# A two-layer hybrid decoder on one core: the products with w1 and w3 by one level of Strassen's scheme, and the first layer's FFN features in two parts

## The chip, the cores and the metric

The kernel runs on one core of a Trainium2 chip. The time is that of one execution on the device in microseconds (us). Engines: PE is TensorE (matrix products), DVE is VectorE, ACT is ScalarE, POOL is GpSimd, SP is SyncE, which issues the transfers (DMAs) between device memory and SBUF. Products land in PSUM.

## What is computed

Two hybrid decoder layers over T = 528 tokens (16 meta tokens and 512 real ones), 1024 features wide. What the change touches is the feed-forward network (FFN) of each layer, 2816 hidden features; the mixing ahead of it (retention, pooling, forgetting attention) stays.

```python
def hybrid_layer(h, w_in, ..., w_out, ln1_g, ln1_b, w1, w3, w2, ln2_g, ln2_b, cos, sin):
    ...
    mix = jnp.einsum('ble,ed->bld', mix, w_out)
    h = layer_norm(ALPHA * h + mix, ln1_g, ln1_b)

    a = jnp.einsum('bld,df->blf', h, w1)
    b = jnp.einsum('bld,df->blf', h, w3)
    y = jnp.einsum('blf,fd->bld', jax.nn.silu(a) * b, w2)
    return layer_norm(ALPHA * h + y, ln2_g, ln2_b)
```

## The kernel before

Activations lie with features on the 128 partitions and tokens along the columns: eight tiles (k = 0 to 7) of 128 features. The tokens are split into half A (272 columns: meta tokens and the first 256) and half B (256). Every fp32 operand is split into a high part (ACT's cast) and a low part (the tile minus its high part, by `sub_lo`, L137 and L138, on DVE or POOL), and a product is three matmuls: high weight with high tile, high with low, low with high (`mm3`, L195 to L197).

Weights come in chunks of 128 x 1024 (512 KB) in the order in which they are used. `fetch` issues the transfer into one of three `raw` buffers; `ensure` has ACT cast it (L174) and DVE or POOL subtract it (L138) into one of four `w` buffers. SP issues all transfers in order.

The FFN's hidden stage (`ffn_hidden`, L973) goes through 22 feature tiles f. Each has two units, one with w1 and one with w3, of eight k tiles each, and each unit is done for half A and half B: 24 matmuls per unit and half. A unit's result is one PSUM buffer `acc`, of which there are two. After a w1 unit ACT takes the Silu (L981); after a w3 unit DVE multiplies (L984), ACT casts the gate to its high part (L986), DVE subtracts the low part. In layer 0 all units go by halves of 272 and 256 columns; in layer 1 the first four units (f = 0 and 1) go by halves of 256, and the rest by 512 columns at once. The first four units do half A before any does half B (A0 to A3, B0 to B3), since half B's layer norm (DVE L334 and L335, ACT L269, casts L271, POOL low parts) is still running when half A's units begin.

After layer 0's hidden stage (262 to 520.6 us of the span) come the products with w2 over all 22 feature tiles, then the second layer norm and layer 1; after layer 1's (885 to 1143 us) the products with w2 for the output (`w2b`). For residual and output the layer norm's result is added up again from its two parts on POOL (`whole`, L355, the operation at L361).

PE's program order is written out: `Plan` picks among pieces by priority and by estimated delays (LAG). The order on the other engines comes from a list scheduler, and every engine runs its queue in order.

Of the kernel before, what the change touches and what calls it, by code (L numbers as in the profile page):

```python
# [43 lines left out]
class Piece:  # L44
    """A run of TensorE work (with what the other engines do on it), placed by Plan."""
# [59 lines left out]
def hymba_kernel(ctx: ExitStack, tc: tile.TileContext, d: dict, out: bass.AP):  # L105
# [16 lines left out]
    # ---------------------------------------------------------------- helpers  # L122
# [17 lines left out]
    # ------------------------------------------------------------ constants in  # L140
# [8 lines left out]
    users = {}  # L149
# [19 lines left out]
    def ensure(upto):  # L169
        while len(loaded) < len(chunks) and len(loaded) <= upto:  # L170
            fetch(len(loaded))
            raw, (_, n, eng) = raws[len(loaded)], chunks[len(loaded)]
            w = wp.tile([P, 2, 1024], F32R, tag="w", name="w")
            nc.scalar.copy(w[:, 0, :n], raw[:, :n])  # L174
# [24 lines left out]
    def unit(u, xs, ks, n, evac, ahead, prio, deps_k):  # L199
        """one output tile: the chunks u of the weights against the tiles xs(), over the k in ks; its last piece."""  # L200
# [3 lines left out]
        for i in range(0, len(ks), q):  # L204
            part = ks[i:i + q]

            def fn(i=i, part=part):
# [13 lines left out]
            for c in {u[k // 8] for k in part}:  # L221
                deps += users.get(c - 4, [])
# [4 lines left out]
            for c in {u[k // 8] for k in part}:  # L227
                users.setdefault(c, []).append(prev)
# [3 lines left out]
    def stage(units, xs, ks, n_of, evac, deps_k, head=0, halves="AB", ahead=2, prio=9):  # L232
        """units: (chunk ids, key); the first `head` units do half A before any does half B.
        Returns the last pieces by (key, half)."""
        done = {}
        i = 0
        while i < len(units):
            g = head if i < head else 1
            for half in halves:
                for u, key in units[i:i + g]:  # L240
# [4 lines left out]
                        lambda k, half=half, key=key: deps_k(half, key, k))  # L245
# [1046 lines left out]
```

## Time and profile before

| | us |
|---|---|
| median of 3 runs | 1273.67 (1272.68 to 1273.88) |
| the profiled execution: its span | 1271.5 |
| that execution with what lies around the span: taken as the median | 1273.7 (2.2 around it) |
| PE busy | 1234.6 |
| DVE, ACT, POOL busy | 646.6, 479.9, 337.7 |

A row of the timeline gives start, duration (us), engine, line, operation, output<-inputs, shape; at its end, in brackets, how long the engine had been idle before it and who released it. A row of windows gives the stretch, its length, then busy time and number of instructions of PE, PE's weight loads, DVE, ACT and POOL, the granted clock of PE, the share of the DMA engines and GB/s. Grouped rows give count, busy time and mean duration in ns; a row of transfers gives count, KB each and the median time from issue to landing. Some matmul records are missing from a trace.

### The profile page before, as it was taken

The page shows a single profiled execution, that of the slowest core. Times are in us where ns is not written, and L with a number is a line of the kernel's source. Part 1 is how long each engine was busy: PE and PEld are TensorE (multiplying, and loading weights), DVE is VectorE, ACT ScalarE, POOL GpSimd, SP SyncE. Part 2 cuts the span into 40 slices and gives each one's busy share as a digit, 9 for nine tenths or more (in the row PEclk, how much of TensorE's full clock was granted, in tenths as well). Part 3 has the DMA queues.
Part 4 walks back from the last instruction along what each step waited for, and adds up shares of the span by engine and source line. Part 5 has one row for each costly group of instructions (what it writes and reads, how often), then busy time and mean ns, then how long its engine had stood idle before and what let it go on. Part 6 is the DMA issues. An engine that isn't in the chain of part 4 may idle for free. (4 is left out here: it accounts for less than half of the span.)

```text
span 1271.5 us, 21413 instructions
## 1 busy us (share of the span) xinstructions
PE 1234.6 (97%) x8650; PEld 1145.8 (90%) x8650; DVE 646.6 (51%) x1257; ACT 479.9 (38%) x893; POOL 337.7 (27%) x375
## 2 busy tenths in 40 slices
PE   7999999889999999999999999998999999999997
PEld 6999989889999999999999899997888888888886
DVE  7575677963333333333384756789632333332226
ACT  5436544543232232222264366455423232221112
POOL 5423339740001100010055243498600000000004
PEclk9999999999999999999999999999899999999999
DMA  6431212423222223233343221134222232222222
GB/s 231 125 99 51 68 34 101 135 98 100 96 88 86 98 84 96 77 90 92 108 143 123 80 80 59 34 118 153 94 84 99 85 99 95 88 100 100 99 91 75
DMA packets 41506, 122.58 MB, mean 96 GB/s; under 512 B 6392, under 2 KB 12696, under 8 KB 41408
## 3 DMA queue, kind: packets, MB, share of 16 engines
q1 hardware_dynamic: 41408, 121.22, 29.1%
q8 instruction: 68, 1.11, 0.4%
q14 instruction: 30, 0.25, 0.1%
HBM read 115.22 MB, written 2.10 MB: 92 GB/s over the span
## 5 line engine op out<-in xcount | busy, mean ns | idle before, releaser
L195 PE MATMUL acc<-xh,w 128*128 128x256 f32 (+2 forms) x1920 | 589.7, 307 | 0.4 <-DVE ka L138 0.4
L196 PE MATMUL acc<-xl,w 128*128 128x256 f32 (+2 forms) x1920 | 582.0, 303 | 1.5 <-POOL xl L138 1.0
L197 PE MATMUL acc<-xh,w 128*128 128x256 f32 (+2 forms) x1920 | 581.8, 303 | 0.0
L138 DVE TENSOR_TENSOR w<-raw,w 128x1024 fp32r<-128x1024 f32 (+1 forms) x181 | 217.4, 1203 | 332.7 <-ACT w L174 332.4
L195 PEld LDWEIGHTS acc<-xh,w 128*128 128x128 f32 x1920 | 363.4, 189 | 18.1 <-issue 1.6
L196 PEld LDWEIGHTS acc<-xl,w 128*128 128x128 f32 x1920 | 364.1, 190 | 16.4 <-POOL xl L138 1.9
L197 PEld LDWEIGHTS acc<-xh,w 128*128 128x128 f32 x1920 | 363.1, 189 | 13.7
L174 ACT CAST w<-raw 128x1024 fp32r<-128x1024 f32 (+1 forms) x211 | 218.8, 1038 | 301.7 <-PE acc L197 121.1
L138 POOL TENSOR_TENSOR w<-raw,w 128x256 fp32r<-128x256 f32 (+1 forms) x74 | 120.6, 1635 | 69.7 <-ACT w L174 61.7
L361 POOL TENSOR_TENSOR y<-xh,xl 128x256 f32<-128x256 f32 (+1 forms) x64 | 51.2, 827 | 225.2 <-DVE g8Bl L138 93.8
L256 POOL TENSOR_TENSOR r<-r,mhalf 128x1 f32<-128x1 f32 (+3 forms) x18 | 14.7, 819 | 324.6 <-DVE r L255 324.6
L138 POOL TENSOR_TENSOR xl<-y,xh 128x256 fp32r<-128x256 f32 (+1 forms) x57 | 49.6, 886 | 22.3 <-ACT xh L271 16.3
L981 ACT ACTIVATE y<-acc 128x272 f32<-128x272 f32 (+1 forms) x44 | 17.2, 392 | 89.0 <-PE acc L197 89.0
L981 ACT ACTIVATE sa<-acc 128x512 f32<-128x512 f32 (+1 forms) x24 | 13.5, 563 | 88.4 <-PE acc L197 88.4
L984 DVE TENSOR_TENSOR sa<-sa,acc 128x512 f32<-128x512 f32 (+1 forms) x24 | 15.4, 642 | 59.0 <-PE acc L197 57.9
L285 DVE SCALAR_TENSOR_TENSOR y<-y,acc 128x256 f32<-128x256 f32 (+1 forms) x48 | 20.1, 420 | 44.5 <-PE acc L197 44.3
L984 DVE TENSOR_TENSOR y<-y,acc 128x272 f32<-128x272 f32 (+1 forms) x44 | 18.9, 429 | 40.4 <-PE acc L197 40.4
L290 POOL TENSOR_TENSOR y<-y 128x256 f32<-128x256 f32 (+1 forms) x12 | 11.0, 914 | 106.3 <-DVE y L285 106.3
L294 ACT ACTIVATE y<-y 128x256 f32<-128x256 f32 (+1 forms) x42 | 17.6, 419 | 54.6 <-DVE y L285 54.5
L680 ACT ACTIVATE p<-p,sm 128x144 f32<-128x144 f32 (+3 forms) x48 | 27.6, 574 | 17.7 <-DVE sm L679 16.1
L683 POOL TENSOR_SCALAR pm<-p,sm 128x16 f32<-128x16 f32 x48 | 21.8, 455 | 43.8 <-DVE sm L681 42.5
L290 DVE TENSOR_TENSOR y<-y 128x256 f32<-128x256 f32 (+1 forms) x30 | 32.1, 1071 | 2.5 <-POOL y L290 1.2
(1000 smaller groups left out, 1916.9 us busy)
## 6 DMA issues: line engine op xcount, KB each, us to landing
raw<-in_w SPq DMA_DIRECT2D x88, 512.0 KB, 3.3
raw<-in_w_in SPq DMA_DIRECT2D x42, 512.0 KB, 4.0
raw<-in_w_out SPq DMA_DIRECT2D x32, 512.0 KB, 3.4
raw<-in_w2b SPq DMA_DIRECT2D x22, 512.0 KB, 3.3
raw<-in_w2a SPq DMA_DIRECT2D x18, 512.0 KB, 3.4
raw<-in_w2a SPq DMA_DIRECT2D x9, 384.0 KB, 3.2
xin<-in_x SPq DMA_DIRECT2D x4, 512.0 KB
out<-y SPq DMA_DIRECT2D x12, 128.0 KB, 1.8
```

Source lines behind the costliest of these rows:

```text
L138: return eng.tensor_tensor(lo, full, hi.bitcast(F32), op=ALU.subtract)
L174: nc.scalar.copy(w[:, 0, :n], raw[:, :n])
L195: nc.tensor.matmul(ps, lhsT=wh, rhs=hi, start=first, stop=False)
L196: nc.tensor.matmul(ps, lhsT=wh, rhs=lo, start=False, stop=False)
L197: nc.tensor.matmul(ps, lhsT=wl, rhs=hi, start=False, stop=last)
L285: nc.vector.scalar_tensor_tensor(y, y, ALPHA, ps, op0=ALU.mult, op1=ALU.add)
L290: (nc.gpsimd if CFG[f"s{i}"] else nc.vector).tensor_tensor(self.s, self.seen[0] if i == 1 else self.s, y, op=ALU.add)
L361: nc.gpsimd.tensor_tensor(y, hi[:, o:].bitcast(F32), lo[:, o:].bitcast(F32), op=ALU.add)
L680: nc.scalar.activation(out=p[:, :NM + nk], in_=p[:, :ce], func=AF.Exp, scale=-1.0, bias=sm[:, 0:1], accum_out=sm[:, 1:2])
L683: nc.gpsimd.tensor_scalar(F[c, "pm"][:, h, :], p[:, :NM], sm[:, 2:3], 1.0, op0=ALU.mult, op1=ALU.mult)
L981: nc.scalar.activation(out=s, in_=ps, func=AF.Silu)
L984: nc.vector.tensor_tensor(s, s, ps, op=ALU.mult)
```

## The change

For feature tiles f = 3 to 21 of both layers, w1 and w3 of one feature tile are taken together as a 2 x 2 block matrix: w1 and w3 are its two rows, the first four and the last four k tiles its columns. The tokens are the second matrix: first and last half of the k tiles by first and last half of the tokens (264 columns each in layer 0, 256 in layer 1). One level of Strassen's scheme (in Winograd's form) makes the four results from seven products of four k tiles each, so 7 x 4 x 3 = 84 matmuls per feature tile where there were 96 of the same width (48 of 512 columns in layer 1).

It needs sums of weights per feature tile (`sums_of`: s1 to s4, with their own high and low parts), sums of tokens once per layer (`factors`: T1 to T4) and sums of products (in `fast`). The seven products lie in three PSUM banks: bank 0 is `acc`, banks 1 and 2 are `one`. Bank 1 is used three times over: product 2 (s2 T2), product 4 (s3 T3) added to it, and product 6 (A22 T4) added to that, each after the reading of what was there.

```diff
+KH = KF // 2
+HEAD = 3
...
+            if eng == "S2":
+                loaded.append(sums_of(raws[len(loaded) - 1], raw, loaded[-1], w))
+                continue
...
+    def sums_of(a1, a2, w1, w2):
...
+        v.tensor_tensor(raw[1], a2[:, a], a2[:, b], op=ALU.add)
+        v.tensor_tensor(raw[2], raw[1], a1[:, a], op=ALU.add)
+        v.tensor_tensor(raw[4], raw[2], a1[:, b], op=ALU.add)
+        v.tensor_tensor(a2[:, a], a2[:, a], a1[:, a], op=ALU.add)
+        for i in (2, 1):
+            nc.scalar.copy(s[i][:, 0], raw[i])
+        nc.scalar.copy(w2[:, 0], a2)
+        nc.scalar.copy(s[4][:, 0], raw[4])
+        sub_lo(v, w1[:, 1], a1, w1[:, 0])
+        for i in (2, 1):
+            sub_lo(v, s[i][:, 1], raw[i], s[i][:, 0])
+        sub_lo(v, w2[:, 1], a2, w2[:, 0])
+        sub_lo(nc.gpsimd, s[4][:, 1], raw[4], s[4][:, 0])
...
+    def factors(k, n, hs, Th, Tl):
...
+        for p, c0, c1 in second(k):
+            v.tensor_tensor(o[1][:, c0:c1], b11[:, c0:c1], p, op=ALU.subtract)
+        for p, c0, c1 in second(k + 4):
+            v.scalar_tensor_tensor(o[0][:, c0:c1], o[1][:, c0:c1], -1.0, p, op0=ALU.mult, op1=ALU.subtract)
+        for (p, c0, c1), (q, _, _) in zip(second(k), second(k + 4)):
+            v.tensor_tensor(o[2][:, c0:c1], q, p, op=ALU.subtract)
+        v.scalar_tensor_tensor(o[3], o[0], -1.0, b21, op0=ALU.mult, op1=ALU.subtract)
+        for i in range(4):
+            nc.scalar.copy(Th[:, k, i], o[i])
+            sub_lo(v if i % 2 else nc.gpsimd, Tl[:, k, i], o[i], Th[:, k, i])
+
+    PRODUCTS = (("A11", "B11", 0), ("s2", "T2", 1), ("s1", "T1", 2), ("s3", "T3", 1), ("A12", "B21", 0), ("A22", "T4", 1),
+                ("s4", "B22", 2))
...
+            def evac(i, f=f, bank=bank, t=t):
+                a, b, c = (bank[j][:, :n] if j in bank else None for j in range(3))
+                if i == 0:
+                    t["p1"], t["u3"] = home(f)
+                    nc.scalar.copy(t["p1"], a)
+                elif i == 1:
+                    t["u2"] = slot(n)
+                    v.tensor_tensor(t["u2"], t["p1"], b, op=ALU.add)
+                elif i == 3:
+                    u = t["u3"]
+                    v.tensor_tensor(u, t["p1"], b, op=ALU.add)
+                    v.tensor_tensor(u, u, c, op=ALU.add)
+                elif i == 4:
+                    t["s"] = slot(n)
+                    nc.scalar.activation(out=t["s"], in_=a, func=AF.Silu)
+                elif i == 5:
+                    v.tensor_tensor(t["p1"], t["p1"], b, op=ALU.add)
+                    gated(f, 0, t["s"], t["p1"])
+                elif i == 6:
+                    v.tensor_tensor(t["u2"], t["u2"], c, op=ALU.add)
+                    nc.scalar.activation(out=t["u2"], in_=t["u2"], func=AF.Silu)
+                    gated(f, 1, t["u2"], t["u3"])
...
+        def split(f, c0, c1, t):
+            hi, lo = (g[:, c0:c1] for g in gt[f])
+            nc.scalar.copy(hi, t)
+            sub_lo(nc.gpsimd if f >= HEAD else nc.vector, lo, t, hi)
...
+        def gated(f, j, s, u):
+            nc.vector.scalar_tensor_tensor(u, s, -1.0, u, op0=ALU.mult, op1=ALU.mult)
+            split(f, N * j, N * (j + 1), u)
...
+        for i, fs in enumerate((range(KH), range(KH, KF))):
...
+            last = fast(l, fs[0 if i else HEAD:], 0, N, Th, Tl, yslot, lambda f: (yslot(N), yslot(N)), gated, [(sums[-1], LAG["T"])], prev)
```

Feature tiles 0 to 2 stay as they were, though in layer 1 all three now go by halves of 256. In layer 0 the hidden stage and its w2 products are cut in two parts: tiles 0 to 10 and their w2 products, then tiles 11 to 21 and theirs, added to the first. Seven chunks more are transferred for the same bytes. The layer norm's results stay in SBUF as fp32, so that `whole` is gone from the FFN. Layer 1's gates are kept as fp32 and split into parts in the last stage, one feature tile at a time.

The order on DVE in a steady part of layer 0, one feature tile before the change (two PSUM readings at L984, the gate's low parts, two weight chunks):

```order
L984 TENSOR_TENSOR y<-y,acc 128x272 [waits PE_49]
L138 TENSOR_TENSOR g13Al<-y,g13Ah 128x272 [waits Activation_49]
L984 TENSOR_TENSOR y<-y,acc 128x256 [waits PE_49]
L138 TENSOR_TENSOR w<-raw,w 128x1024 [waits DMAHW5_49,Activation_49]
L138 TENSOR_TENSOR g13Bl<-y,g13Bh 128x256 [waits Activation_49]
L138 TENSOR_TENSOR w<-raw,w 128x1024 [waits DMAHW6_49,PE_49,Activation_49]
```

The same after the change, most of a feature tile: L1068 is the reading of product 6, L1071 of product 7, L1059 of the next tile's product 2; L1135 are the gates, L140 the low parts (`w` of A11 with A12 and of s3 with A22, `S` of s1 and s2), L192 to L195 the weight sums. The row behind the last one is L1062, the reading of the next tile's product 4.

```order
L1068 TENSOR_TENSOR y<-y,one 128x264 [waits PE_49]
L140 TENSOR_TENSOR w<-raw,w 128x1024 [waits Activation_49]
L1135 SCALAR_TENSOR_TENSOR y<-y 128x264 [waits DVE_49]
L140 TENSOR_TENSOR w<-raw,w 128x1024 [waits Activation_49]
L1071 TENSOR_TENSOR y<-y,one 128x264 [waits PE_49]
L140 TENSOR_TENSOR S<-sr,S 128x512 [waits Activation_49]
L1135 SCALAR_TENSOR_TENSOR y<-y 128x264 [waits Activation_49]
L1059 TENSOR_TENSOR y<-y,one 128x264 [waits PE_49]
L192 TENSOR_TENSOR sr<-raw 128x512 [waits DMAHW1_49,DVE_49]
L140 TENSOR_TENSOR S<-sr,S 128x512 [waits Activation_49]
L195 TENSOR_TENSOR raw<-raw 128x512 [waits DMAHW0_49,DVE_49]
L193 TENSOR_TENSOR sr<-sr,raw 128x512 [waits DVE_49]
```

Where six instructions stood per feature tile, fifteen stand, five of which read PSUM for PE's next product. POOL, which had nothing per tile there, gets two low parts of gates and that of s4 in layer 0, and that of s4 alone in layer 1.

At the head of layer 0's hidden stage, ACT's order before around the Silu of unit A2 (y_3568; the xh rows are half B's high parts, g0Ah the high part of the first gate):

```order
L986 CAST g0Ah_3329<-y_3461 128x272 [waits DVE_49]
L269 ACTIVATE y_2657<-y_2657,c_pv_96 128x256 [waits DVE_49]
L269 ACTIVATE y_2659<-y_2659,c_pv_96 128x256 [waits DVE_49]
L271 CAST xh_84<-y_2657 128x256 [waits Activation_49]
L981 ACTIVATE y_3568<-acc_3538 128x272 [waits PE_49]
L269 ACTIVATE y_2661<-y_2661,c_pv_96 128x256 [waits DVE_49]
```

The same Silu after the change (y_3580); Th are the high parts of T1 to T4:

```order
L1029 CAST Th_3329<-y_3484 128x264 [waits DVE_49]
L1029 CAST Th_3329<-y_3487 128x264 [waits DVE_49]
L1029 CAST Th_3329<-y_3504 128x264 [waits DVE_49]
L1029 CAST Th_3329<-y_3503 128x264 [waits DVE_49]
L1029 CAST Th_3329<-y_3505 128x264 [waits DVE_49]
L1029 CAST Th_3329<-y_3506 128x264 [waits DVE_49]
L1029 CAST Th_3329<-y_3523 128x264 [waits DVE_49]
L1029 CAST Th_3329<-y_3524 128x264 [waits DVE_49]
L1029 CAST Th_3329<-y_3522 128x264 [waits DVE_49]
L1109 ACTIVATE y_3580<-acc_3550 128x272 [waits PE_49,Pool_49]
L1029 CAST Th_3329<-y_3525 128x264 [waits DVE_49]
```

It has moved from the middle of half B's layer norm to behind all of it and fourteen casts of T. PE's order there is as before; the first unit of half B takes the `acc` buffer that this Silu reads:

```order
L228 MATMUL acc_3582<-xh_84,w_3559 128x272
L226 MATMUL acc_3615<-xh_84,w_3264 128x256 [waits Activation_49]
L227 MATMUL acc_3615<-xl_85,w_3264 128x256 [waits Pool_49]
L228 MATMUL acc_3615<-xh_84,w_3264 128x256
L226 MATMUL acc_3615<-xh_84,w_3264 128x256
```

The first row is the end of unit A3, the second the first matmul of B0. On PE nothing has moved here; what its wait stands for has.

More of the change, by code (lines that the diff above doesn't have):

```diff
@@ L230, in unit, with stage @@
         return prev
-    def stage(units, xs, ks, n_of, evac, deps_k, head=0, halves="AB", ahead=2, prio=9):
+    def stage(units, xs, ks, n_of, evac, deps_k, head=0, halves="AB", ahead=2, prio=9, k0=0):
         done = {}
@@ L965, in mixing @@
             ap = norm.finish([done[m, half] for m in range(KD)], base, base + 8, xn)
-            om.holds("y", KD, ap[-1])
+            keep[half] = [Piece(None, 0.0, [], 0) for _ in range(2)]
+            for p in keep[half]:
+                om.holds("y", KD // 2, p)
             for k in range(KD):
@@ L974, in ffn_hidden @@
+    def ffn_hidden(l, slot, put):
         sa = {}
@@ new lines, in put, with room @@
+        def put(f, half, s, ps):
+            nc.vector.tensor_tensor(s, s, ps, op=ALU.mult)
+            split(f, *((0, NA) if half == "A" else (NA, T)), s)
+        def gated(f, j, s, u):
+            nc.vector.scalar_tensor_tensor(u, s, -1.0, u, op0=ALU.mult, op1=ALU.mult)
+            split(f, N * j, N * (j + 1), u)
+        def room(fs):
+            for f in fs:
+                gt[f] = [gp.tile([P, T], F32R, tag=f"g{f % KH}{s}", name=f"g{f}{s}") for s in "hl"]
+        room(range(KH))
+        us, evac = ffn_hidden(l, yslot, put)
@@ L1005, in ffn_mid @@
-        end = [done[us[-1][1], h] for h in "AB"]
-        us, dn = list(zip(w2_u[l], (*range(KD), KD - 2))), {}
-        norm = {h: Norm(h, n_of[h], hs, f"f{l}") for h in "AB"}
-        for part, halves in ((us[:6], "AB"), (us[6:7], "A"), (us[7:8], "AB"), (us[8:], "B")):
-            dn.update(stage(part, lambda half: [gt[f, half] for f in range(KF)], list(range(KF)), lambda h, key: n_of[h],
-                            lambda m, half, ps: norm[half].evac(m, ps),
-                            lambda half, key, k: [gdone[k, half], wh] + end, halves=halves, ahead=1))
+        sums = [plan.add(lambda k=k: factors(k, N, hs, Th, Tl), 0.0, [ready["A", KD - 1][0], ready["B", KD - 1][0]], 5) for k in range(4)]
@@ new lines, in ffn_mid, with evac2 @@
+        gdone = {f: [(done[(f, 1), h], LAG["g"]) for h in "AB"] for f in range(HEAD)}
+        prev = done[us[-1][1], "B"]
+        dn = {}
+        norm = {h: Norm(h, n_of[h], hs, f"f{l}", 1.0) for h in "AB"}
+        def evac2(m, half, ps):
+            y = hs[half][m]
+            nc.vector.scalar_tensor_tensor(y, y, ALPHA, ps, op0=ALU.mult, op1=ALU.add)
+        for i, fs in enumerate((range(KH), range(KH, KF))):
+            if i:
+                prev = plan.add(lambda: room(range(KH, KF)), 0.0, end, 9)
+            last = fast(l, fs[0 if i else HEAD:], 0, N, Th, Tl, yslot, lambda f: (yslot(N), yslot(N)), gated, [(sums[-1], LAG["T"])], prev)
+            gdone.update({f: [(p, LAG["g2"])] for f, p in last.items()})
+            end = [last[fs[-1]]]
+            us = list(zip(w2_u[i], (*range(KD), KD - 2)))
+            for part, halves in ((us[:6], "AB"), (us[6:7], "A"), (us[7:8], "AB"), (us[8:], "B")) if i else ((us, "AB"),):
+                dn.update(stage(part, lambda half, fs=fs: {f: tuple(g[:, :NA] if half == "A" else g[:, NA:] for g in gt[f]) for f in fs},
+                                list(fs), lambda h, key: n_of[h],
+                                lambda m, half, ps, i=i: norm[half].evac(m, ps) if i else evac2(m, half, ps),
+                                lambda half, key, k, end=end: gdone[k] + end, halves=halves, ahead=1, k0=fs[0]))
+            end = [dn[us[-1][1], h] for h in "AB"]
@@ L1029, in ffn_last @@
                      lambda half, key, k: [ready[half, k]], head=4)
-        done.update(stage(us[4:], lambda half: both, list(range(KD)), lambda h, key: 2 * NB, evac,
-                          lambda half, key, k: [ready[h, k] for h in half], halves=("AB",)))
-        ht, hw = {}, {}
+        sums = [plan.add(lambda k=k: factors(k, NB, hw, Th, Tl), 0.0, [ready["A", KD - 1][0], ready["B", KD - 1][0]], 5) for k in range(4)]
+        last = fast(l, range(HEAD, KF), NM, NB, Th, Tl, sa, lambda f: (g[f][:, :NB], g[f][:, NB:]), gated, [(sums[-1], LAG["T"])], done[us[-1][1], "B"])
@@ L1034, in turn @@
+        ht = {}
         def turn(half, b, q):
-            if b == 0 and q == 0:
-                hw[half] = whole(x, half, 256)
             tp = one()
@@ L1071, in part @@
             nc.tensor.matmul(ps, lhsT=lo, rhs=wh, start=False, stop=last_)
+        for k in range(3):
+            split(k)
         KT = 4
         for k in range(KF - KT):
-            ensure(w2_u[l][k][0] + 2)
+            ensure(w2_u[-1][k][0] + 2)
+            split(k + 3)
             for b in range(4):
@@ L1083, in ffn_last @@
             nc.sync.dma_start(gb[j], d["gb"][:, j, :])
-        fo = [gp.tile([P, 512], F32, tag="sa", name="fo", bufs=3) for _ in range(2)]
+        fo = [gp.tile([P, 512], F32, tag="sr", name="fo", bufs=3) for _ in range(2)]
         def sums(b, st, q):
```

197 lines of the change are left out of this document (133 added, 64 removed).

## The prediction

> **What bounds the kernel now.** I read the page's table of engines first, then the row of granted clock, then the windows of the two hidden stages that the change touches.
>
> ```profile
> span 1271.5 us, 21413 instructions
> PE 1234.6 (97%) x8650; PEld 1145.8 (90%) x8650; DVE 646.6 (51%) x1257; ACT 479.9 (38%) x893; POOL 337.7 (27%) x375
> PEclk9999999999999999999999999999899999999999
> ...
> 250.00:520.00 270.00, 266.46 (x2168) 265.64 (x2168) 107.44 (x165) 87.51 (x155) 31.12 (x34) 0.99 0.28 93
> 900.00:1140.00 240.00, 240.00 (x1123) 198.01 (x1122) 85.19 (x101) 77.24 (x121) 14.80 (x18) 1.00 0.28 92
> ```
>
> TensorE (PE) is busy for 97% of the span at full clock, and in the two FFN hidden stages for 266.46 of 270 us and for all of 240 us (first pair of figures of a window). VectorE (DVE) is at 107.44 and 85.19 us there. So fewer matmuls shorten these stages, but only until VectorE, which gets the new additions, is late instead. What a matmul costs is read from the Silu instructions, one after each w1 unit:
>
> ```profile
> 301.22 0.40 ACT L981 ACTIVATE y<-acc 128x272 f32<-128x272 f32 x1 [1.62 <-PE acc L197]
> 304.05 0.39 ACT L981 ACTIVATE y<-acc 128x256 f32<-128x256 f32 x1 [2.43 <-PE acc L197]
> 312.93 0.40 ACT L981 ACTIVATE y<-acc 128x272 f32<-128x272 f32 x1 [1.62 <-PE acc L197]
> ...
> 922.61 0.60 ACT L981 ACTIVATE sa<-acc 128x512 f32<-128x512 f32 x1 [4.23 <-PE acc L197]
> 933.73 0.60 ACT L981 ACTIVATE sa<-acc 128x512 f32<-128x512 f32 x1 [4.01 <-PE acc L197]
> ```
>
> Layer 0: 312.93 - 301.22 = 11.71 us for one feature tile, that is 96 matmuls of 272 and 256 columns, 0.122 us each at a mean of 264. The 24 matmuls of 256 columns between the first two rows take 2.83 us, 0.118 each. Layer 1: 11.12 us for 48 matmuls of 512 columns, 0.232 each.
>
> **What the change removes.** For 19 of 22 feature tiles per layer, 84 matmuls of 264 (layer 0) or 256 columns (layer 1) stand for 96. That is 84 x 0.122 = 10.25 us, 1.46 less; and 84 x 0.118 = 9.91 us, 1.21 less. If TensorE never waits: 19 x 1.46 + 19 x 1.21 = 50.7 us. Feature tile 2 of layer 1 stays plain but moves to 256 columns: 96 x 0.118 - 11.12 = 0.2 us dearer. The two parts of w2 hold the same matmuls, and the seven more SP transfers move the same bytes; I cost both at nothing, since the weights for them are prepared under products that last longer than their casts (up to 1 us at each of two joints if not).
>
> The PSUM banks make one chain per feature tile. Product 6 (A22 T4) needs bank 1, which VectorE must have read after product 4 (L1062); the next thing that VectorE does for TensorE waits for product 6 (L1068); and until the next L1062 it has thirteen instructions in its order, L1068 itself among them: four of 264 columns that read PSUM, two gates of 264 in SBUF, two subtractions of 1024, five operations of 512. Their durations:
>
> ```profile
> 311.03 1.23 DVE L138 TENSOR_TENSOR w<-raw,w 128x1024 fp32r<-128x1024 f32 x1 [0.70 <-ACT w L174]
> 312.17 0.42 DVE L138 TENSOR_TENSOR g3Bl<-y,g3Bh 128x256 fp32r<-128x256 f32 x1
> ...
> 930.38 0.68 DVE L138 TENSOR_TENSOR g2l<-sa,g2h 128x512 fp32r<-128x512 f32 x1
> ...
> 272.02 0.43 DVE L138 TENSOR_TENSOR g0Al<-y,g0Ah 128x272 fp32r<-128x272 f32 x1
> 272.37 0.41 DVE L335 TENSOR_TENSOR y<-y,one 128x256 f32<-128x256 f32 x1
> 272.70 0.41 DVE L334 TENSOR_TENSOR y<-y,one 128x256 f32<-128x256 f32 x1
> ```
>
> In a queue the next instruction starts 0.08 us before the end of the one ahead (311.03 + 1.23 against 312.17). So 1024 columns cost 1.14, 512 cost 0.60, 264 cost 0.34 (0.35 at 272, 0.33 at 256). Sum: 6 x 0.34 + 2 x 1.14 + 5 x 0.60 = 7.3 us, and 0.4, my estimate, for dependent neighbours and extra semaphores. Then product 6: 12 x 0.122 = 1.46, and from its last matmul to a reader:
>
> ```profile
> 312.60 0.29 PE L197 MATMUL acc<-xh,w 128*128 128x272 f32 x1
> ...
> 910.58 0.38 ACT L981 ACTIVATE sa<-acc 128x256 f32<-128x256 f32 x1
> ...
> 911.01 0.38 PE L195 MATMUL acc<-xh,w 128*128 128x256 f32 x1
> ```
>
> The Silu of 312.93 starts 0.33 us after its last matmul starts, 0.20 after that one's turn of 0.122; and a matmul starts 0.05 us after the reader that it waits for (910.58 + 0.38 against 911.01). The loop so far: 7.7 + 1.46 + 0.25 = 9.4 us in layer 0 and 9.3 in layer 1, **shorter than TensorE's 10.25 and 9.91**. What decides is GpSimd (POOL), which gets three subtractions per tile in layer 0 (264, 264 and 512 columns) and one of 512 in layer 1:
>
> ```profile
> 910.65 2.44 POOL L361 TENSOR_TENSOR y<-xh,xl 128x256 f32<-128x256 f32 x2
> 911.34 1.75 POOL L361 TENSOR_TENSOR y<-xh,xl 128x256 f32<-128x256 f32 x1
> ...
> 910.71 1.78 DVE L138 TENSOR_TENSOR w<-raw,w 128x1024 fp32r<-128x1024 f32 x1 [3.40 <-ACT w L174]
> 912.41 0.41 DVE L984 TENSOR_TENSOR sa<-sa,acc 128x256 f32<-128x256 f32 x1
> 912.74 1.43 DVE L138 TENSOR_TENSOR w<-raw,w 128x1024 fp32r<-128x1024 f32 x1
> ...
> 270.27 0.75 POOL L138 TENSOR_TENSOR xl<-y,xh 128x256 fp32r<-128x256 f32 x1 [5.05 <-ACT xh L271]
> L138 POOL TENSOR_TENSOR w<-raw,w 128x1024 fp32r<-128x1024 f32 x28 | 68.8, 2460 | 13.0 <-ACT w L174 13.0
> ```
>
> Beside GpSimd a VectorE subtraction of two SBUF tiles took 1.78 and 1.43 us instead of 1.23, and GpSimd's own took 1.75 instead of 0.75. The second GpSimd row ends at 913.09, 0.60 after VectorE's 912.49: they take turns, and a turn of GpSimd is 0.60 for 256 columns. VectorE's L984 between them, which reads PSUM, kept its 0.41. With 0.75 for 256 and 2.46 for 1024, GpSimd's 512 is about 1.3, its turn about 1.15 (estimate). In layer 0 that is 0.61 + 0.61 + 1.15 = 2.4 us per tile, in layer 1 1.15. How much lies beside VectorE's four PSUM readings, no row shows: between nothing and all of it is added. A reading is 0.34 long and a turn 0.6 or more, so at most half of a small turn hides behind one; I take 1.8 and 1.15 as exposed. **Loops: 11.2 us in layer 0, 10.5 in layer 1** (ends 10.25 to 11.8, 9.91 to 10.7; weight transfers add to layer 1's upper end, since w chunks landing after 4.0 instead of 3.3 us come late for L192 by up to 0.4).
>
> ```profile
> raw<-in_w SPq DMA_DIRECT2D x88, 512.0 KB, 3.3
> raw<-in_w_in SPq DMA_DIRECT2D x42, 512.0 KB, 4.0
> ```
>
> The loop holds only where weights are prepared two tiles ahead: 15 tiles of layer 0, 17 of layer 1; the last two of each of the three runs of tiles go at TensorE's rate. Saved: 15 x 0.5 + 4 x 1.46 + 17 x 0.6 + 2 x 1.21 = 26 us, less 0.2 for tile 2 and about 1.5 where the runs fill: **24 us**.
>
> **What it adds.** T1 to T4 are made at the head of each hidden stage, between the layer norm's last steps for half B. Before, that head runs without a stop:
>
> ```profile
> 268.35 0.42 DVE L335 TENSOR_TENSOR y<-y,one 128x256 f32<-128x256 f32 x1 [1.95 <-PE one L329]
> ...
> 272.13 0.40 ACT L981 ACTIVATE y<-acc 128x272 f32<-128x272 f32 x1
> ...
> 274.83 0.29 PE L197 MATMUL acc<-xh,w 128*128 128x272 f32 x1
> 274.95 0.28 PE L195 MATMUL acc<-xh,w 128*128 128x256 f32 x1
> ```
>
> The Silu at 272.13 reads unit A2 and frees the PSUM buffer that the first unit of half B takes at 274.95. In the changed order fourteen casts of T stand ahead of this Silu on ACT, the last of them behind VectorE's 15 PSUM operations (0.33), 12 of 256 columns and 9 of about 264 (0.34) and nine small ones (estimate 0.1): 5.0 + 4.1 + 3.1 + 0.9 = 13.1, with 1.0 for dependent neighbours 14 us from 268.35, so 282.4, then cast and Silu (0.4 each) and 0.25: B starts at 283.4 at the earliest, 8.5 us late. GpSimd has about 13 subtractions in that time, 0.6 a turn, 7.8 if none hides: 16 us late at most. I take 12. What is queued behind the Silu on ACT are g1's cast, the next weight cast and B's Silus, and TensorE waits for all of them through that one buffer. A stop costs clock as well:
>
> ```profile
> 892.00:896.00 4.00, 4.00 (x17) 3.71 (x18) 2.34 (x8) 0.38 (x1) 1.17 (x2) 0.50 0.31 118
> 896.00:900.00 4.00, 4.00 (x28) 3.95 (x27) 2.67 (x8) 0.55 (x2) 4.00 (x7) 0.78 0.00 0
> ...
> 891.95 0.66 PE L312 MATMUL one<-c_ident,y 128*128 128x128 f32 x2 [4.24 <-DVE y L290]
> ```
>
> After 4.24 us of idle the granted clock (seventh figure) was 0.50 for 4 us and 0.78 for 4 more: 4 x 0.5 + 4 x 0.22 = 2.9 us lost; I take 2.5. In layer 1 the A2 Silu keeps its early place, but B0's Silu (910.58 before) comes behind eleven T casts and a weight cast. The same VectorE work from 899 gives 912.5, with turns and casts about 914; B2 starts 3.5 us late (1 to 6), and half a clock step after it, 1.5. Heads together: 12 + 2.5 + 3.5 + 1.5 = **19.5 us** (11 to 28). The 32 additions that GpSimd no longer makes (L361) and the splitting of layer 1's gate inside the last stage lie beside TensorE either way, and I cost them at nothing.
>
> **Sum.** 1271.5 + 2.2 around it is the median of 1273.7. 1273.7 - 24 + 19.5 = **1269**, own range 1260 to 1280, chance 0.50.
>
> **Rivals.** *TensorE stays the bound* (0.22): at most 0.85 us of GpSimd's turns is exposed in layer 0, 0.6 in layer 1, the rest beside PSUM readings and waits. Then 1273.7 - 50.5 + 19.5 = 1243. For it: the unslowed 0.41 of 912.41. Against: nine of the loop's thirteen instructions, the longest among them, read two SBUF tiles.
>
> *VectorE and GpSimd queue for each other in full* (0.20), the slower side: a turn is GpSimd's whole duration, 0.75 + 0.75 + 1.3 = 2.8 in layer 0 and 1.3 in layer 1, none hidden; loops 12.2 and 10.6; saved -7.4 + 5.8 + 8.8 + 2.4 - 1.7 = 8; the layer 0 head stops 16 us: 1273.7 - 8 + 23.5 = 1289. It decides against the change from loops of about 11.3 and 10.7 on, where 24 falls to 19.5. For it: 1.78 instead of 1.23 from a single GpSimd operation; against: the 0.60 above. The Trainium skill (SBUF — State Buffer, Who interferes with whom) calls the pair of ports that these two share an exclusive lock, held for the whole instruction, and taken by a VectorE instruction with two SBUF inputs; by that rule this rival is the forecast, 1289, and the rows bear out the turns but not their full length.
>
> *Matmuls in three banks go slower than in one* (0.03): at 0.14 us each 84 of them take the old 11.7, so only the cost stays, 1293. Against it: 512 columns cost 0.232 and 256 cost 0.118, so the pitch goes by columns. The Trainium skill (TensorE: Matmul & The Clock Gate, Back-to-back issue gap) gives 131 ns sustained for 512 columns and 81 for 128, by which halves would be much dearer in layer 1 than 512; this trace has 232 and 118 and decides against it.
>
> **How the numbers follow.** 0.05 is left for what I have not seen, on either side. Range 1243 to 1288: it keeps the forecast, half of the first rival and half of the second. A measurement of this kernel tells about 0.2%, 2.5 us, from no change: faster means under 1271.1. Faster: 0.22, 0.28 of the forecast's 0.50 and 0.02, so 0.52. Same: 0.14 of the forecast and 0.01, so 0.15. Slower: the rest, 0.33.
>
> **What would show it.** The spacing of L1056 or L1066 in the new trace: 11.2 and 10.5 for me, 10.25 and 9.91 for the first rival, 12.2 and 10.6 for the second. VectorE's L140 of 1024 above 1.23 where GpSimd's L140 falls. TensorE's idle time should lie at product 6, released by VectorE's L1062, and in one piece of some 12 us ahead of the first matmul of half B in layer 0, released by ACT. If TensorE waits mostly elsewhere (products 3 or 4, or weights), my chain is wrong.

## The result, and the profile after

| | before | after |
|---|---|---|
| median, us | 1273.78 (1272.68 to 1274.23) | 1284.16 (1283.70 to 1287.78) |
| ratio | | 1.0091 (95%: 1.0077 to 1.0106) |
| span of the profiled execution | 1271.5 | 1282.4 |

In brackets behind a median stand the fastest and the slowest run. The change makes the kernel 0.9% **slower**. The page of the changed kernel, its rows of engines and two of its costliest groups (busy time, mean ns, then the idle time of PE just ahead of them and what ended it):

```profile
span 1282.4 us, 23349 instructions
PE 1201.0 (94%) x9154; PEld 1145.8 (89%) x9154; DVE 909.1 (71%) x1738; ACT 579.4 (45%) x1102; POOL 429.1 (33%) x437
...
L226 PE MATMUL acc<-xh,w 128*128 128x256 f32 (+1 forms) x1024 | 301.4, 294 | 16.4 <-ACT y L1109 12.5
...
L1087 PE MATMUL one<-Th,w 128*128 128x264 f32 (+1 forms) x608 | 127.0, 291 | 23.0 <-DVE y L1062 13.1
```

TensorE is busy for 33.6 us less (1201.0 against 1234.6) and idle for 44.5 us more. The busy time falls by less than the 50.7 us of the prediction in part because matmuls behind a wait count longer (0.58 us for the first row of the stops below) and the mean granted clock is lower (0.986 against 0.994). Most of the added idle time has the two causes that the prediction named: 12.5 us in one piece behind ACT's L1109, and 23.0 us ahead of the products with T, mostly behind VectorE's L1062.

To see where it was lost, I cut both spans at four places of TensorE's row that both kernels have: the first transposes of half B's layer norm ahead of layer 0's FFN, the last w2 product of layer 0, the first transposes of layer 1's mixing, and half B's layer norm ahead of layer 1's FFN. The rows at the two inner cuts, before and after:

```profile
650.95 0.28 PE L197 MATMUL acc<-g21Bh,w 128*128 128x256 f32 x1
...
667.94 0.38 PE L570 MATMUL one<-c_ident,y 128*16 128x128 f32 x2
```

```profile
655.49 0.28 PE L228 MATMUL acc<-g21h,w 128*128 128x256 f32 x1
658.09 0.41 PE L346 MATMUL one<-c_ident,y 128*128 128x128 f32 x2 [2.33 <-DVE y L324]
...
678.77 0.49 PE L604 MATMUL one<-c_ident,y 128*16 128x128 f32 x3
```

| stretch, us | before | after | difference | predicted |
|---|---|---|---|---|
| up to layer 0's FFN | 260.04 | 261.04 | +1.0 | 0 |
| layer 0: half B's layer norm to the last w2 product | 390.9 | 394.5 | +3.5 | about +2 |
| from there to the transposes of layer 1's mixing | 17.0 | 23.3 | **+6.3** | 0 |
| the mixing of layer 1 | 224.0 | 224.4 | +0.4 | 0 |
| layer 1: half B's layer norm to the end | 379.6 | 379.3 | -0.3 | **about -7** |
| sum | 1271.5 | 1282.4 | +10.9 | -4.7 |

The first stretch is the same work in both; over the runs below it ends between 260.4 and 263.7 us, so its 1.0 is no result. Two stretches went wrong: one that I had costed at nothing, and layer 1.

The stops at the two heads, TensorE's rows in the changed kernel (the first matmul of half B in layer 0, and that of its third unit in layer 1):

```profile
288.58 0.58 PE L226 MATMUL acc<-xh,w 128*128 128x256 f32 x1 [12.48 <-ACT y L1109]
...
925.03 0.39 PE L226 MATMUL acc<-xh,w 128*128 128x256 f32 x1 [3.15 <-ACT sa L1109]
```

Both are released by the Silu that the prediction named.

The loop itself is as forecast in kind. One feature tile of layer 1 on VectorE, from the reading of product 4 to the next one, with TensorE's product 6 and GpSimd's only instruction of that tile:

```profile
1028.01 0.41 DVE L1062 TENSOR_TENSOR g<-g,one 128x256 f32<-128x256 f32 x1
...
1030.19 0.42 DVE L1068 TENSOR_TENSOR g<-g,one 128x256 f32<-128x256 f32 x1 [0.84 <-PE one L1087]
1030.53 1.22 DVE L140 TENSOR_TENSOR w<-raw,w 128x1024 fp32r<-128x1024 f32 x1
1031.66 0.42 DVE L1195 SCALAR_TENSOR_TENSOR g<-sa,g 128x256 f32<-128x256 f32 x1
1032.00 1.22 DVE L140 TENSOR_TENSOR w<-raw,w 128x1024 fp32r<-128x1024 f32 x1
1033.13 0.41 DVE L1071 TENSOR_TENSOR sa<-sa,one 128x256 f32<-128x256 f32 x1
1033.46 0.69 DVE L140 TENSOR_TENSOR S<-sr,S 128x512 fp32r<-128x512 f32 x1
1034.07 0.42 DVE L1195 SCALAR_TENSOR_TENSOR g<-sa,g 128x256 f32<-128x256 f32 x1
1034.47 0.42 DVE L1059 TENSOR_TENSOR sa<-g,one 128x256 f32<-128x256 f32 x1
1035.41 0.69 DVE L192 TENSOR_TENSOR sr<-raw 128x512 f32<-128x512 f32 x1 [0.52 <-DMA raw<-in_w]
1036.02 0.68 DVE L140 TENSOR_TENSOR S<-sr,S 128x512 fp32r<-128x512 f32 x1
1036.62 0.68 DVE L195 TENSOR_TENSOR raw<-raw 128x512 f32<-128x512 f32 x1
1037.22 1.77 DVE L193 TENSOR_TENSOR sr<-sr,raw 128x512 f32<-128x512 f32 x1
1038.92 0.41 DVE L1062 TENSOR_TENSOR g<-g,one 128x256 f32<-128x256 f32 x1
...
1036.66 1.78 POOL L140 TENSOR_TENSOR S<-sr,S 128x512 fp32r<-128x512 f32 x1 [9.13 <-ACT S L199]
...
1039.38 0.38 PE L1087 MATMUL one<-Th,w 128*128 128x256 f32 x1 [0.66 <-DVE g L1062]
```

The loop takes 1038.92 - 1028.01 = 10.91 us. Two things in it are not VectorE's own work: L193 takes 1.77 instead of 0.68, since it stands across GpSimd's low part of s4 (1.09), and L192 waits 0.52 for a transfer. Without them it is 9.30, the 9.3 of the prediction. In layer 0 a tile takes 11.49 us (L1062 at 354.91 and 366.40): three VectorE instructions are longer by 0.23, 0.57 and 1.10 beside GpSimd's three, together 1.90 where I took 1.8, and the transfer costs 0.28; 9.3 is left there too.

```profile
360.44 0.91 DVE L140 TENSOR_TENSOR S<-sr,S 128x512 fp32r<-128x512 f32 x1
...
362.92 1.25 DVE L140 TENSOR_TENSOR S<-sr,S 128x512 fp32r<-128x512 f32 x1
364.09 1.78 DVE L195 TENSOR_TENSOR raw<-raw 128x512 f32<-128x512 f32 x1
```

### The profile page after: what moved, and what is told of

It reads as the page before. It is cut to its first block, busy times and chain, and to the rows that moved or that the text cites. A ratio compares the mean times of both kernels' runs of the same rounds, so it can differ in the third digit from the quotient of the medians.

```text
span 1282.4 us, 23349 instructions
## 1 busy us (share of the span) xinstructions
PE 1201.0 (94%) x9154; PEld 1145.8 (89%) x9154; DVE 909.1 (71%) x1738; ACT 579.4 (45%) x1102; POOL 429.1 (33%) x437
## 5 line engine op out<-in xcount | busy, mean ns | idle before, releaser
L226 PE MATMUL acc<-xh,w 128*128 128x256 f32 (+1 forms) x1024 | 301.4, 294 | 16.4 <-ACT y L1109 12.5
L227 PE MATMUL acc<-xl,w 128*128 128x256 f32 (+1 forms) x1024 | 294.1, 287 | 2.6 <-POOL xl L140 2.1
L228 PE MATMUL acc<-xh,w 128*128 128x256 f32 (+1 forms) x1024 | 293.3, 286 | 0.0
L140 DVE TENSOR_TENSOR w<-raw,w 128x1024 fp32r<-128x1024 f32 (+2 forms) x188 | 216.5, 1158 | 52.1 <-ACT w L179 52.0
L226 PEld LDWEIGHTS acc<-xh,w 128*128 128x128 f32 x1024 | 196.6, 192 | 20.2 <-ACT y L1109 12.7
L227 PEld LDWEIGHTS acc<-xl,w 128*128 128x128 f32 x1024 | 196.8, 192 | 4.3 <-POOL xl L140 3.6
L228 PEld LDWEIGHTS acc<-xh,w 128*128 128x128 f32 x1024 | 196.4, 192 | 0.0
L140 POOL TENSOR_TENSOR S<-sr,S 128x512 fp32r<-128x512 f32 x38 | 59.7, 1572 | 273.3 <-ACT S L199 242.0
L1087 PE MATMUL one<-Th,w 128*128 128x264 f32 (+1 forms) x608 | 127.0, 291 | 23.0 <-DVE y L1062 13.1
L140 POOL TENSOR_TENSOR w<-raw,w 128x256 fp32r<-128x256 f32 (+1 forms) x74 | 122.1, 1656 | 70.6 <-ACT w L179 62.5
L1087 PEld LDWEIGHTS one<-Th,w 128*128 128x128 f32 x608 | 100.3, 191 | 30.0 <-DVE y L1062 16.1
L1087 PE MATMUL acc<-xh,w 128*128 128x264 f32 (+1 forms) x608 | 121.9, 283 | 0.0
L1087 PE MATMUL one<-Th,S 128*128 128x264 f32 (+1 forms) x608 | 116.9, 285 | 0.0
L1087 PEld LDWEIGHTS acc<-xh,w 128*128 128x128 f32 x608 | 99.2, 189 | 0.0
L1087 PEld LDWEIGHTS one<-Th,S 128*128 128x128 f32 x608 | 97.1, 190 | 0.0
L140 DVE TENSOR_TENSOR S<-sr,S 128x512 fp32r<-128x512 f32 x76 | 63.6, 839 | 0.5 <-ACT S L197 0.3
```

The lines of the kernel that those rows point to most:

```text
L140: return eng.tensor_tensor(lo, full, hi.bitcast(F32), op=ALU.subtract)
L226: nc.tensor.matmul(ps, lhsT=wh, rhs=hi, start=first, stop=False)
L227: nc.tensor.matmul(ps, lhsT=wh, rhs=lo, start=False, stop=False)
L228: nc.tensor.matmul(ps, lhsT=wl, rhs=hi, start=False, stop=last)
L1087: nc.tensor.matmul(ps, lhsT=a[:, w], rhs=b, start=fresh and k == 0 and q == 0, stop=k == 3 and q == 2, skip_group_check=True)
```

## The experiments

The question after this was threefold: whether the loop is the chain over bank 1 or simply too much work on VectorE and GpSimd; whether the stop at layer 0's head is T's place in the queues; and what the 6.3 us between the layers are. Each experiment edits the kernel after the change; where edits are put together, the text says so. Of each edit only the main lines are shown. "Layer 0" and "layer 1" in the tables are the second and the last stretch of the table above.

**T later.** T of one k at a time is made after half B's units of tiles 0 and 1.

```diff
-        sums = [plan.add(lambda k=k: factors(k, N, hs, Th, Tl), 0.0, [ready["A", KD - 1][0], ready["B", KD - 1][0]], 5) for k in range(4)]
+        sums = [plan.add(lambda k=k: factors(k, N, hs, Th, Tl), 0.0, [ready["A", KD - 1][0], ready["B", KD - 1][0], done[(k // 2, k % 2), "B"]], 5) for k in range(4)]
```

> T1 to T4 are made one k at a time after the first four units of half B (T of k = 0 and 1 after the two units of tile 0, of k = 2 and 3 after those of tile 1), in both layers, so that the Silus of units A2 (layer 0) and B0 (layer 1) stand ahead of most casts of T on ACT. Theory (the stop of 12.8 us ahead of half B in layer 0 and those of 1.1 and 3.4 us in layer 1 come from these Silus' place in ACT's queue, and the T work itself finds room beside the units): the stops go, with about 2 us of clock: 1284 - 17 - 2 = 1265 us; TensorE's pause ahead of the first matmul of half B under 0.5 us in layer 0. Rival (VectorE's T work is the limit wherever it stands): half B's units or the first fast tile wait instead, and the time stays above 1278.

1281.19 us (1279.06 to 1282.59), ratio 1.0063 (1.0048 to 1.0078): the rival. TensorE, ACT and GpSimd at the place to which the stop moved:

```profile
303.41 0.59 PE L226 MATMUL acc<-xh,w 128*128 128x272 f32 x1 [7.47 <-ACT y L1109]
...
302.31 0.75 ACT L1029 CAST Th<-y 128x264 fp32r<-128x264 f32 x2 [2.90 <-DVE y L1026]
302.97 0.39 ACT L1109 ACTIVATE y<-acc 128x272 f32<-128x272 f32 x1
...
286.71 4.67 POOL L140 TENSOR_TENSOR Tl<-y,Th 128x264 fp32r<-128x264 f32 x1 [2.05 <-ACT Th L1029]
```

Half B begins on time, but the w3 unit of tile 2 is 7.5 us late: the Silu that frees its buffer stands behind casts of T that wait for VectorE, which from 282 to 305 us has hardly a pause. In layer 1 nothing moved. So the order alone is not it: T and the weight sums of the first fast tiles are more than VectorE can do in the time of three plain tiles.

**Half B's units last.** In layer 0's second w2 part, half A does tiles 4 to 7 and then half B 7, 4, 5, 6.

```diff
-            for part, halves in ((us[:6], "AB"), (us[6:7], "A"), (us[7:8], "AB"), (us[8:], "B")) if i else ((us, "AB"),):
+            for part, halves in ((us[:4], "AB"), (us[4:7], "A"), (us[7:8], "AB"), (us[8:], "B")) if i else ((us, "AB"),):
```

> In layer 0's second w2 part half A's units of tiles 4, 5, 6, 7 come first and then half B's 7, 4, 5, 6 (three more weight loads of two chunks), so that four units of half B instead of two lie behind the end of half A. Theory (the mixing of layer 1 starts about 6 us later than before because a unit of w2 is now half as long, 33 matmuls for 66, and two of them hide only half of half A's layer norm): 1284 - 6 = 1278 us, and TensorE's pause of 2.6 us at the end of w2 in layer 0 goes. Rival (the layer norm itself is slower, or the mixing is late for weights): within 1 us of 1284, or slower by the added loads.

1281.61 us (1280.77 to 1285.12), ratio 1.0065 (1.0048 to 1.0082). The stretch between the layers is 20.8 us instead of 23.3: 2.5 back, not 6. The pause of 2.33 us at the end of w2 is gone, but these came in the mixing:

```profile
661.98 0.39 PE L227 MATMUL acc<-xl,w 128*128 128x272 f32 x1 [1.61 <-POOL xl L140]
...
664.80 0.60 PE L227 MATMUL acc<-xl,w 128*128 128x272 f32 x1 [2.19 <-POOL xl L140]
```

Half A's layer norm had twice the cover and was late nevertheless. My reading, which no run tests by itself, is this: under a unit of 33 matmuls VectorE, ACT and GpSimd have a chunk of weights, a reading of the unit and the layer norm's sums to do, as under 66 before.

**The two parts alone.** Layer 0 is plain, without T and without the seven products; only its two parts stay.

```diff
-        us = list(zip(w13_u[l], [(f, w) for f in range(HEAD) for w in range(2)]))
+        us = list(zip(w13_u[l], [(f, w) for f in range(HEAD if l else KF) for w in range(2)]))
```

> Layer 0 without the seven products (all 22 tiles plain, no T), but with its hidden stage and w2 in two parts as the change has them; layer 1 as changed. Theory (the two parts of w2 by themselves cost 6.3 us between the end of w2 and the mixing of layer 1, since a unit of w2 has half the matmuls to hide the layer norm and the weights): from the last w2 matmul to the first transposes of layer 1's mixing 23 us as in the change, 17.0 before; with layer 1 at about its old time, 1273 + 6 = 1279 to 1280 us. Rival (the delay comes with the seven products, whose kept tiles and busier VectorE make the layer norm late): that stretch back at 17 to 18 us, 1273 us.

1279.75 us (1279.52 to 1281.51), ratio 1.0052 (1.0037 to 1.0067). The end of w2 and the transposes of layer 1's mixing:

```profile
651.73 0.28 PE L228 MATMUL acc<-g21h,w 128*128 128x256 f32 x1
654.34 0.41 PE L346 MATMUL one<-c_ident,y 128*128 128x128 f32 x2 [2.33 <-DVE y L324]
...
675.01 0.27 PE L604 MATMUL one<-c_ident,y 128*16 128x128 f32 x1
```

675.01 - 651.73 = 23.3 us, the same as with the seven products. Layer 0's own stretch is 390.8, as before the change (390.9). So the 6.3 us come with the two parts of w2 (the halved units, and the residual kept in SBUF that goes with them), and the loss there is not Strassen's. The windows of this stretch, before and in the change:

```profile
650.95:667.94 16.99, 15.95 (x120) 14.98 (x118) 14.73 (x34) 9.23 (x23) 10.92 (x19) 1.00 0.53 174
...
655.49:678.77 23.28, 18.00 (x119) 16.40 (x118) 20.10 (x46) 15.05 (x36) 18.31 (x27) 0.93 0.44 143
```

TensorE has the same matmuls to do in both. It is idle for 5.3 us instead of 1.0, and busy for 2.05 us longer, at a granted clock of 0.93 instead of 1.00: about a third of the 6.3 us is matmuls that run slower behind the pauses.

**The loop: low parts on VectorE, and a bank for product 6.** Two edits, alone and together.

```diff
-            sub_lo(nc.gpsimd if f >= HEAD else nc.vector, lo, t, hi)
+            sub_lo(nc.vector, lo, t, hi)
...
-        sub_lo(nc.gpsimd, s[4][:, 1], raw[4], s[4][:, 0])
+        sub_lo(v, s[4][:, 1], raw[4], s[4][:, 0])
```

> The low parts of the gates and of s4 of the fast tiles are made by VectorE instead of GpSimd (three more VectorE instructions per tile in layer 0, one in layer 1; GpSimd has nothing in the loop). Theory (the turns of GpSimd, 1.9 us per tile in layer 0 and 1.1 in layer 1, make the loop longer than TensorE's time): tiles at 10.3 to 10.5 us in layer 0 instead of 11.5 and 9.9 to 10.4 in layer 1 instead of 11.1; 15 x 1.1 + 17 x 0.9 = 32, so about 1252 us. Rival (what counts is VectorE's sum of work, and the turns only fill its waits): the added 1.3 and 0.6 us lengthen the loop, 1284 or more.

```diff
-    PRODUCTS = (("A11", "B11", 0), ("s2", "T2", 1), ("s1", "T1", 2), ("s3", "T3", 1), ("A12", "B21", 0), ("A22", "T4", 1),
+    PRODUCTS = (("A11", "B11", 0), ("s2", "T2", 1), ("s1", "T1", 2), ("s3", "T3", 1), ("A12", "B21", 0), ("A22", "T4", 3),
...
-                    u = t["u3"]
-                    v.tensor_tensor(u, t["p1"], b, op=ALU.add)
-                    v.tensor_tensor(u, u, c, op=ALU.add)
+                    v.tensor_tensor(t["p1"], t["p1"], b, op=ALU.add)
+                    v.tensor_tensor(t["u3"], t["p1"], c, op=ALU.add)
```

> Product 6 goes into a PSUM bank of its own instead of into bank 1 behind product 4 (the sum of products 1, 2 and 4 is kept, and product 6 added to it: as many VectorE instructions). Theory (the loop over bank 1, product 6 waiting for the reading of product 4, sets the tile's time): without it the bound is VectorE's sum, 8.3 + 1.9 + 0.5 = 10.7 to 11 us in layer 0 and 9.9 to 10.3 in layer 1: 15 x 0.6 + 17 x 0.9 = 24, so about 1260 us. Rival (VectorE with GpSimd's turns is the bound by itself, or the transfers): tiles stay at 11.4 and 11.0, 1282 us.

> Both together: product 6 in a bank of its own, and all low parts of the fast tiles' loop on VectorE. Theory (with neither GpSimd's turns nor the chain over bank 1, TensorE is the bound again): tiles at 10.25 to 10.4 us in layer 0 (10.7 with the low parts alone moved) and 9.95 to 10.2 in layer 1 (10.35): 15 x 0.35 + 17 x 0.25 = 10 less, 1252 us. Rival (VectorE's sum, 8.3 + 1.3 + waits, or the weights' landing is what is left): as with the low parts alone, 1262 us.

| | us | ratio (95%) | layer 0 | layer 1 |
|---|---|---|---|---|
| the change | 1284.16 | 1.0091 (1.0077 to 1.0106) | 394.5 | 379.3 |
| low parts on VectorE | 1262.19 | 0.9916 (0.9899 to 0.9933) | 384.4 | 366.7 |
| product 6 in its own bank | 1265.77 | 0.9942 (0.9927 to 0.9957) | 385.6 | 369.8 |
| both | 1255.82 | 0.9865 (0.9848 to 0.9881) | 380.1 | 365.3 |

Each edit alone goes the way of its theory, for less than it put (32 and 24): 22.0 and 18.4 us. Together they give 28.3 and not 40.4: both take from the same excess, since the loop is long only where the chain over bank 1 and the turns of GpSimd on it come together. That three more VectorE instructions per tile (0.34 + 0.34 + 0.60 us) make layer 0 ten us faster is the clearest sign of what the turns cost (1.9). The spacing of the copies of product 1 (L1056), tiles 11 to 20 in layer 0 and tiles 3 to 20 in layer 1, in the change:

```profile
468.20 0.37 ACT L1056 COPY y<-acc 128x264 f32<-128x264 f32 x1
570.85 0.38 ACT L1056 COPY y<-acc 128x264 f32<-128x264 f32 x1 [0.53 <-PE acc L1087]
945.28 0.37 ACT L1056 COPY g<-acc 128x256 f32<-128x256 f32 x1 [0.33 <-PE acc L1087]
1134.88 0.37 ACT L1056 COPY g<-acc 128x256 f32<-128x256 f32 x1 [0.75 <-PE acc L1087]
```

and with both edits:

```profile
463.45 0.37 ACT L1056 COPY y<-acc 128x264 f32<-128x264 f32 x1
556.72 0.38 ACT L1056 COPY y<-acc 128x264 f32<-128x264 f32 x1 [0.89 <-PE acc L1086]
930.72 0.38 ACT L1056 COPY g<-acc 128x256 f32<-128x256 f32 x1 [0.78 <-PE acc L1086]
1106.35 0.37 ACT L1056 COPY g<-acc 128x256 f32<-128x256 f32 x1 [0.75 <-PE acc L1086]
```

In the change these are (570.85 - 468.20) / 9 = 11.4 and (1134.88 - 945.28) / 17 = 11.2 us a tile, with both edits 10.4 and 10.3 (layer 1 has the transposes for the output in some of its tiles, before the change too). Tiles that wait for nothing take 10.23 and 10.02 (the last spacings of the two layers in the change, 570.85 to 581.08 and 1134.88 to 1144.90): with both edits 23 of the 35 spacings inside the runs of tiles lie within 0.1 us of these. There TensorE is the bound again, and the rival, that the transfers or VectorE's sum are what is left, falls for these tiles.

**T's low parts on VectorE too**, on top of the first of these two edits.

```diff
-            sub_lo(v if i % 2 else nc.gpsimd, Tl[:, k, i], o[i], Th[:, k, i])
+            sub_lo(v, Tl[:, k, i], o[i], Th[:, k, i])
```

> As x_lock, and the low parts of T1 and T3 too on VectorE instead of GpSimd. Theory (VectorE needs 20 us for 14 us of work at the head, since it takes turns with GpSimd's low parts of T): eight more VectorE instructions of 0.34 cost 2.7 us, the turns of 0.6 that go save 4.8: the stop ahead of half B in layer 0 shrinks from 12.8 to about 10.5, those in layer 1 from 4.5 to about 2.5: 1262 - 4 = 1258 us. Rival (the turns at the head fall beside PSUM readings): the stops grow by up to 2.7 each, 1266 us.

1258.69 us (1258.16 to 1259.43), ratio 0.9884 (0.9869 to 0.9899), about as expected. The first matmul of half B in layer 0, and the one that waited 3.15 us in layer 1:

```profile
288.34 0.58 PE L226 MATMUL acc<-xh,w 128*128 128x256 f32 x1 [11.12 <-ACT y L1109]
...
912.11 0.39 PE L226 MATMUL acc<-xh,w 128*128 128x256 f32 x1 [0.98 <-ACT sa L1109]
```

Eight more VectorE instructions, and the stop is 1.4 us shorter in layer 0 (12.48 before); layer 1's stretch is 363.9 us instead of 366.7.

**More plain tiles to make T in.** Layer 0 keeps five plain tiles, and T of one k is made after half B's first unit of tiles 0, 1, 2 and 3.

```diff
+HEADS = (5, 3)
...
+        sums = [plan.add(lambda k=k: factors(k, N, hs, Th, Tl), 0.0, [ready["A", KD - 1][0], ready["B", KD - 1][0], done[((0,0),(1,0),(2,0),(3,0))[k], "B"]], 5) for k in range(4)]
```

> The change as it is, but layer 0 keeps five plain tiles instead of three and makes T for one k at a time after the first half B unit of tiles 0, 1, 2 and 3. Theory (layer 0's stop of 12.8 us is T's work ahead of half B's units in VectorE's and ACT's queues, too much for the time of three plain tiles): the stop goes, 12.8 us and 2 of clock, and the two more plain tiles cost 2 x (11.7 - 11.5) to 2 x 1.46: the stretch from half B's layer norm to the last w2 product in layer 0 goes from 394.5 to about 381, the time from 1284 to about 1271. Rival (the T work is only moved on, as when it stood behind two tiles): stops of together 7 us stay, 1278 us.

1270.10 us (1266.90 to 1274.29), ratio 0.9978 (0.9968 to 0.9988). Layer 0's stretch is 381.9 us instead of 394.5, and TensorE has no pause over 0.6 us between half B's layer norm and the first fast tile. The theory's number was 381. So the stop was T's work in too little time, and it is worth 12.6 us with the clock behind it, net of what two more plain tiles cost. (The profiled execution is the slowest of ten: its first stretch, the same work, took 2.1 us more than in the change.)

**Together.** First four plain tiles in both layers with T as in the first experiment; then layer 0 as just above and layer 1 with three plain tiles. Both have all low parts on VectorE, product 6 in its own bank and half B's units of w2 last.

> Four plain tiles per layer instead of three, T after the first units of half B, low parts on VectorE, product 6 in its own bank, and half B's units of w2 in layer 0 last. Theory (the T work, some 12 us of VectorE, needs the 8 us that VectorE has free in a plain tile, and then nothing stops at layer 0's head): 1252 from the two loop edits, 2 less for w2, 12 less for the stop in layer 0, 2.7 more for the fourth plain tile in both layers: 1241 us. Rival (the stop only moves, as it did with three plain tiles): 1250 us.

1245.55 us (1244.74 to 1246.42), ratio 0.9781 (0.9766 to 0.9795): better than both kernels, though one stop of 6.0 us stayed in layer 0, in tile 2 again.

> The same in layer 0, with all low parts on VectorE, product 6 in its own bank and half B's units of w2 last; layer 1 with three plain tiles. Theory: against the version with four plain tiles (1245.6 us), the stop of 6.3 us in layer 0 goes with some 2 us of clock, one more plain tile costs 1.5 us, layer 1 gains 1.2 with one plain tile less: 1240 us. Rival (VectorE is full until the fast tiles begin wherever T stands): 1245 us.

1239.34 us (1238.68 to 1240.82), ratio 0.9735 (0.9722 to 0.9748). The stop is gone, and layer 0's stretch is 370.4 us. This is the best version: 2.65% faster than before, with the same seven products.

A fourth buffer for raw weights, which might take the transfer out of the loop, was not tried.

## Why the prediction was wrong

The sign was wrong: 10.4 us more instead of 4.7 less. That the time lies inside the range is owed to the range's width, which took in half of the second rival, and not to the sum. By the stretches, the change came out 15.6 us dearer than forecast (10.9 more instead of 4.7 less), in round numbers: 6.3 at the end of w2, 6.7 in layer 1, 1.5 in layer 0, and the rest in the stretches that do the same work.

- *What TensorE saves* per tile was right: 84 matmuls at 0.122 and 0.118 us. Tiles without waits are spaced 10.2 and 10.0 us.
- *The loop* was right as a mechanism: product 6 waits for L1062, and giving it another bank takes 18.4 us off. Base (9.3 us) and GpSimd's turns (1.90 for 1.8 in layer 0, 1.09 for 1.15 in layer 1) came out as put. **The mis-sized term is the transfer**: I took it as hidden and put only up to 0.4 us for it into layer 1's upper end. The buffer comes free with the end of L140 at 1031.75 and L192 starts at 1035.41: 3.66 us (the median landing before was 3.3), while VectorE has only 3.1 us of other work in between. The landing stood in the trace of before, and the other work could be added up from its rows. The wait costs 0.52 in the layer 1 tile shown and 0.28 in the layer 0 tile; over 36 tiles, the first of each run among them, VectorE waited 21.2 us there, and 9.3 of these in 16 steady tiles of layer 1, 0.58 each (below). This is read from the rows; no run took the transfer away by itself. So the loops were 11.5 us for 11.2 and 10.9 for 10.5 in the tiles shown, beyond the 11.3 and 10.7 from which, by the prediction's own count, the change does not pay. In layer 1 the 17 tiles took 11.2 on the mean where plain ones with the same transposes had taken 11.3, and the heads ate the rest. One spacing of 13.7 us is in that mean, where a transfer came 1.96 us late (L192 at 1103.56); without it the mean is 11.0.

```profile
L192 DVE TENSOR_TENSOR sr<-raw x38: 680/693/1647, 299.7 to 1126.3; 128x512 f32<-128x512 f32 x38
...
  DMA raw<-in_w: 21.2, 36
...
  DMA raw<-in_w: 9.3, 16
```

The first row gives the count and the shortest, median and longest ns of L192, the second how long VectorE was idle ahead of it for a transfer, and how often; the third is the same from 950 to 1130 us alone.

- *The heads* were right: 12.5 us of stop in layer 0 for 12, 3.15 in layer 1 for 3.5 (925.03, behind ACT's L1109), and the 12.6 that more plain tiles gave back (net of their own cost) for 12 + 2.5. The clock behind the stops cost about 1.5 us in layer 0 (0.62 granted over the next 4 us) for 2.5, and 1.7 in layer 1 (0.69 over 4 us, then 0.88 over 4) for 1.5. The cause named, T's casts ahead of the Silu, is the place where it shows; the experiments put the weight on VectorE's work, since making T later among the same three plain tiles only moved the stop (7.47 us), and giving VectorE more plain tiles removed it.
- **The step that failed outright** is "the two parts of w2 hold the same matmuls ... I cost both at nothing". The matmuls are the same, but that stretch is 6.3 us longer, shown by the two parts alone: 4.2 of pauses and about 2 of slower matmuls behind them. The reason that fits is that a unit is half as long, and half B's two units behind half A's end hide half as much of its layer norm, with as many readings and weights per unit. I looked at the joints from tiles to w2 and not at the end of w2, where TensorE's cover was needed. Giving half A's layer norm its old length of cover gave back 2.5, so the cover is part of it; what holds the rest stays open, though GpSimd's low parts of half A end the waits there.
- *The rivals*: TensorE as the bound did not come, and comes with the two loop edits. VectorE and GpSimd queueing in full (1289) had the right side but too long turns: 1.09 us for 512 columns, not 1.3, and its spacings of 12.2 and 10.6 us did not come. Matmuls in three banks are not slower: 84 of them take 10.23 us where nothing waits.

## What to carry to other kernels

Fewer matmuls pay only as far as the slowest chain that returns to them: write it down as a loop, with every engine's turn and every buffer's refill in it, and compare it with TensorE's time before counting the saving. A split that leaves the sum of work alone can still halve what each unit hides, so look at what stood under the last units. Where two engines take turns for SBUF, moving work to the busier one can be faster.

## What was not expected of the hardware

GpSimd does not always get its turn. In the steady loop of layer 0 an instruction of 264 columns took 1.1 to 1.2 us (one of 256 took 0.75 before the change), but while VectorE ran two-input SBUF instructions back to back at the head, one took 4.67 us (286.71 in the first experiment). And a 512 KB transfer, 3.3 us from issue to landing in the median before the change, once left VectorE idle for 1.96 us (L192 at 1103.56 in the change).
